# RWKV-7's triangular inverses: layouts turned on VectorE instead of through DRAM, with a new order and new engines around them

## The chip, the cores and the metric

One core of a Trainium2 chip runs the whole program. The metric is the device time of one execution in microseconds (us); a kernel's time is the median of its runs. The profile comes from one further execution, with its own time.

## What is computed

Two blocks of two layers each, in 32-bit floats: 512 tokens, 1024 features. The first layer, and only that one is touched here, joins a convolution branch `ya` and an RWKV-7 branch `yb`:

```python
z = h @ even_w_in
a_val, a_glu, a_gate, r, k, v, wd, ad, b_gate = split_cols(z, EVEN_SIZES)
ya = conformer_conv(a_val, a_glu, ...) * silu(a_gate)   # 31 taps, layer norm over 1024 features
yb = rwkv7_mix(r, k, v, wd, ad, ...) * silu(b_gate)     # 16 heads of 64
out = concatenate([ya, yb], axis=-1) @ even_w_out
x = x + gate[:, None, :] * out

def rwkv7_step(state, inp):                             # scanned over the 512 tokens
    r_t, w_t, k_t, v_t, kk_t, a_t = inp
    sa = einsum('bhvk,bhk->bhv', state, -kk_t)
    state = state * w_t + sa * (kk_t * a_t) + v_t * k_t
    y = einsum('bhvk,bhk->bhv', state, r_t)
```

After it come a sparse attention layer, an LRU layer and a forgetting attention layer, which stay as they are.

## The kernel before

**Projections.** Nearly all of TensorE's work is weight products. Each 128x128 weight tile times 128x512 activations is done as three matmuls, by a high and a low part of both factors (`mm3`, L168 to L170): `wh` times `h` (the activations' high part), `wh` times their low part, `wl` times `h`. The raw tile `wr` comes by an SP DMA (L133). ScalarE makes `wh` (L145) and minus `wr` (L146), and a DMA on POOL's queue adds `wr` in memory to give `wl` (L147). `wh` and `wl` have four buffers each. `K.fill` yields such products in steps of three matmuls, so that they can be laid between other work.

**The RWKV branch** is a scan over 8 chunks of 64 tokens, for 8 heads at a time: half 0 (H0), then half 1 (H1). Each half has four stages. `prep` makes decayed queries and keys `AR` and `BK`. `inverse` needs, for each of the 64 pairs of head and chunk, the inverse of a unit triangular 64x64 matrix. `merge` puts its blocks together. `chunk`, eight times, carries the state on; TensorE gets projections to do beside it.

**The inverse** (L656 on). TensorE makes the 64x64 products N (L669, four PSUM banks). VectorE multiplies each bank by the mask `gmask` (L671) and the result goes to DRAM. From there DMAs bring the two 32x32 diagonal blocks of each matrix back as `Nu`, with matrices along the partitions (L675), and the block off the diagonal as `No` (L677). VectorE then solves by forward substitution in 31 steps, each a product and a sum in two pieces (L688, L689): a chain in which each instruction needs the last. The solution `Yu` goes to DRAM. A copy of its first 64 partitions, blocks transposed (L691), goes there as well. From DRAM, `merge` loads `Yt` (L703) and `X11` (L705) in the layout that TensorE needs: rows of a block along the partitions. All these DMAs are on SP's queue. Then come, for 32 matrices at a time, 32x32 products (L714), a ScalarE copy (L717), further products (L719) and a copy into `Yt` (L720).

**Around it.** `ahead` prepares a chunk's matrices: masked products G (L729, L731), V transposed (L736, L739), and for all chunks but the last the keys scaled by the decay `PC`, one POOL product of 128x512 (L745), four TensorE transposes and a ScalarE copy (L748, L750). `conv_stats` (L880 on), laid beside H1's inverse, subtracts the mean from eight tiles (POOL, L888), squares them (ScalarE, L890), sums the squares (POOL, L894), and multiplies the sum by ones for the deviation (L898, L899; reciprocal L904). Beside it, the products of the finished `yb` with `even_w_out` run as a fill (evacuated at L964), for which `yb` is split into high and low parts (L971, and on POOL L972). The other half, the products with `ya`, needs H1's merge behind it in TensorE's order.

**What sets the order.** The program is written in one order, and a scheduler of the tile framework reorders it by a simulated timeline and by priorities (`K.later` lowers the priority of what stands in it, `issue_after` ties it behind an instruction). Tiles come from pools with a count of buffers per tag (`q4` has three here). Engines run their own instructions in the order that results, and wait on semaphores.

Of the kernel before, what the change touches and what calls it, by code (L numbers as in the profile page):

```python
# [10 lines left out]
F = mybir.dt.float32  # L11
# [4 lines left out]
OP = mybir.AluOpType  # L16
# [443 lines left out]
def even_layer(K, ada1):  # L460
# [12 lines left out]
    with K.layer("even", {"mm": (0, 1), "t": (2, 3, 4), "u": (5, 6), "ada": (7,), "py": (7,)}, s=6, k=4, v=4, q4=3, no=1, Yt=1, BKt=2, SAV=2, U=3, cu=2, fg=3, mean=2, awa=1, pa=1):  # L473
        xT, hT = [], []
        ss = SumSq(K, tags=("s", "cu"), eng=nc.vector)
        for i in range(ND):
# [89 lines left out]
        class Half:  # L566
# [91 lines left out]
            def inverse(self):  # L658


                AR, BK = self.AR, self.BK
                No, Nu = K.t("no", (P, 4 * NCH, 32)), K.t("q4", (P, 32, 32))
                n = K.name("sp")
                nd = K.dram.tile([P, 4 * NCH, C], F, name=n, tag=n)
                for j in range(4):
                    p = K.ps("t")
                    for c in range(NCH):
                        for b in range(2):
                            mm(p[hs(b), c * C:(c + 1) * C], lhsT=BK[hs(b), j, c, b], rhs=AR[hs(b), j, c, 0], start=True, stop=True)  # L669
                    n = K.t(shape=(P, NCH, C))  # L670
                    nc.vector.tensor_tensor(out=n, in0=v3(p), in1=gmask[:, None, 0:C].to_broadcast([P, NCH, C]), op=OP.mult)  # L671
                    nc.sync.dma_start(out=nd[:, NCH * j:NCH * j + NCH], in_=n)
                quarters = [(b, q, 64 * b + 32 * q, slice(64 * q + 32 * b, 64 * q + 32 * b + 32)) for b in range(2) for q in range(2)]
                for b, q, r, o in quarters:
                    nc.sync.dma_start(out=Nu[o], in_=nd[r:r + 32, :, 32 * q:32 * q + 32].rearrange("a u b -> u a b"))  # L675
                    if q == 0:
                        nc.sync.dma_start(out=No[r:r + 32], in_=nd[r:r + 32, :, 32:64])  # L677
                Yu, pr = K.t("q4", (P, 32, 32)), K.t("q4", (P, 32, 32))
                nc.gpsimd.memset(Yu, 0.0)
                nc.gpsimd.memset(Yu.rearrange("p a b -> p (a b)")[:, 0::33], 1.0)  # L680

                for b in range(31):
                    for eng, r0, r1 in ((nc.vector,0,8),(nc.vector,8,32)):
                        if b >= r0:
                            a = slice(r0, min(b + 1, r1))
                            sh = [P, a.stop - r0, 31 - b]
                            z = pr[:, a, b + 1:]
                            eng.tensor_tensor(out=z, in0=Yu[:, a, b:b + 1].to_broadcast(sh), in1=Nu[:, b:b + 1, b + 1:].to_broadcast(sh), op=OP.mult)  # L688
                            eng.tensor_tensor(out=Yu[:, a, b + 1:], in0=Yu[:, a, b + 1:], in1=z, op=OP.add)  # L689
                Yd = K.spill(Yu)  # L690
                self.last = nc.vector.tensor_copy(pr[0:64], Yu[0:64].rearrange("p a b -> p b a"))  # L691
                Xd = K.spill(pr[0:64])
                self.ahead(0, K.t("SAV", (P, 2, 4, C)))
                self.parts = No, Yd, Xd, quarters

            def merge(self, fill=()):

                No, Yd, Xd, quarters = self.parts
                Yt = self.Yt = K.t("Yt", (P, 4 * NCH, C))
                X11 = K.t("q4", (P, 4 * NCH, 32))  # L700
                for b, q, r, o in quarters:
                    f = lambda d, o: d[o].rearrange("u a b -> a u b")
                    nc.sync.dma_start(out=Yt[r:r + 32, :, 32 * q:32 * q + 32], in_=f(Yd, o))  # L703
                    if q == 0:
                        nc.sync.dma_start(out=X11[r:r + 32], in_=f(Xd, o))  # L705
                    else:
                        nc.gpsimd.memset(Yt[r:r + 32, :, 0:32], 0.0)
                for u in range(0, 4 * NCH, 16):
                    p, p2 = K.ps("t"), K.ps("t")
                    o1 = K.t(shape=(P, 16, 32))  # L710
                    for b in range(2):
                        r, r2 = slice(64 * b, 64 * b + 32), slice(64 * b + 32, 64 * b + 64)
                        for c in range(16):
                            i = mm(p[r2, 32 * c:32 * c + 32], lhsT=No[r, u + c], rhs=X11[r, u + c], start=True, stop=True)  # L714
                        if fill:
                            K.steps(fill, 2, i.ins)
                        nc.scalar.copy(o1[r2], p[r2].rearrange("p (c t) -> p c t", t=32))  # L717
                        for c in range(16):
                            mm(p2[r, 32 * c:32 * c + 32], lhsT=o1[r2, c], rhs=Yt[r2, u + c, 32:64], start=True, stop=True)  # L719
                        nc.scalar.copy(Yt[r, u:u + 16, 32:64], p2[r].rearrange("p (c t) -> p c t", t=32))  # L720

            def ahead(self, c, SAV):
# [18 lines left out]
                if c < NCH - 1:  # L741

                    bk = K.t(shape=(P, 4, P))
                    pcb = self.PC[:, :, c].unsqueeze(2).to_broadcast([P, 4, P])
                    nc.gpsimd.tensor_tensor(out=bk, in0=BK[:, :, c].rearrange("p j a t -> p j (a t)"), in1=pcb, op=OP.mult)  # L745
                    p = K.ps("t")
                    for j in range(4):
                        nc.tensor.transpose(p[:, j * P:(j + 1) * P], bk[:, j], K.ident)  # L748
                    BKt = K.t("BKt", (P, 8, C))
                    nc.scalar.copy(BKt, v3(p))  # L750
# [127 lines left out]
        def conv_stats():  # L878
# [77 lines left out]
        with K.later():  # L956
# [706 lines left out]
```

## Time and profile before

| | |
|---|---|
| Median of 3 runs | 1786.72 us (1777.45 to 1789.82) |
| The profiled execution's own time | 1791.05 us |
| its span, first to last instruction | 1789.3 us |
| TensorE busy | 1657.9 us (93%) |
| VectorE / ScalarE / POOL busy | 1142.2 / 1090.4 / 637.6 us |
| mean granted TensorE clock | 0.955 of full |

TensorE is busy for nearly all of the span, so what is not its own work is found as its gaps, and as the stretches in which it is granted a lower clock. All times inside the span count from its start. In a row of the timeline, the bracket at the end is the time that the engine sat idle before the instruction and what ended it. A row with xN stands for N instructions in sequence.

### The profile page before, as it was taken

To read this page: it belongs to the slowest core of one execution; us is meant where nothing else is said; L and a number is where in the kernel's file an instruction comes from. 1 tells how busy PE (TensorE), PEld (TensorE's weight loads), DVE (VectorE), ACT (ScalarE), POOL (GpSimd) and SP (SyncE) were. 2 spreads that over 40 slices of the span, in tenths; PEclk is the share of its full clock that TensorE was granted. 3 is DMA by queue.
4 is the path that set the end of the run, shared out by engine and by line. 5 is a ranking of instruction groups with operands and counts; after the bars stand their busy time and mean duration, and the time that the engine had idled before them with its cause. 6 is when DMAs were issued, how large, how long until landed. Compare 5 with 4: busy or idle time off the path is not lost.

```text
span 1789.3 us, 26544 instructions
## 1 busy us (share of the span) xinstructions
PE 1657.9 (93%) x9250; PEld 1310.1 (73%) x9250; DVE 1142.2 (64%) x2247; ACT 1090.4 (61%) x2106; POOL 637.6 (36%) x678
## 2 busy tenths in 40 slices
PE   5899999998995999888999899999999999999997
PEld 4676777776664777767887688888788777877775
DVE  6489776795948567456968878922688621454442
ACT  3574545445554435478565678765789755776775
POOL 1244423233566212133323445332333333333332
PEclk9899997898998989899999999999999999999999
DMA  9866894446678976476879741078777798865654
GB/s 284 211 147 163 184 215 110 107 95 174 153 179 193 273 219 151 119 170 142 179 168 229 197 89 35 18 166 193 165 177 167 150 190 190 199 143 138 154 109 116
DMA packets 164087, 289.19 MB, mean 162 GB/s; under 512 B 43985, under 2 KB 60753, under 8 KB 162929
## 3 DMA queue, kind: packets, MB, share of 16 engines
q0 software_dynamic: 60352, 107.24, 35.7%
q1 hardware_dynamic: 99568, 172.91, 30.9%
q10 hardware_dynamic: 4032, 7.34, 1.1%
q8 instruction: 73, 1.20, 0.3%
q14 instruction: 62, 0.50, 0.1%
HBM read 162.10 MB, written 18.12 MB: 101 GB/s over the span
## 4 chain that ended last, share of the span: by engine, by line
PE 59%; DVE 13%; DMA 12%; issue 8%; ACT 3%; POOL 3%; SPq 1%; POOLq 0%; DVEq 0%; ACTq 0%
PE ps L168 15%; PE ps L169 15%; PE ps L170 15%; DVE x L859 4%; DMA wl<-wr 3%; DMA wr<-in_even_w_in 2%; POOL wl L147 1%; DMA adm<-in_ada_w 1%; PE ps L1525 1%; PE ps L729 1%; DMA sp<-gt 1%; PE ps L1521 1%; PE ps L550 1%; PE ps L1261 1%; POOL mean L894 1%
## 5 line engine op out<-in xcount | busy, mean ns | idle before, releaser
L147 POOL DMA_DIRECT2D wl<-wr x416 | 364.7, 882 | 871.6 <-ACT wl L146 772.3
L170 PE MATMUL ps<-h,wl 128*128 128x512 f32 x1240 | 498.8, 406 | 29.4 <-DMA wl<-wr 29.0
L168 PE MATMUL ps<-h,wh 128*128 128x512 f32 x1240 | 508.5, 415 | 18.7 <-ACT h L332 6.8
L169 PE MATMUL ps<-h,wh 128*128 128x512 f32 x1240 | 500.0, 405 | 0.1
L145 ACT CAST wh<-wr 128x512 fp32r<-128x512 f32 (+1 forms) x416 | 251.9, 606 | 355.6 <-PE ps L169 253.8
L170 PEld LDWEIGHTS ps<-h,wl 128*128 128x128 f32 x1240 | 241.0, 195 | 91.0 <-DMA wl<-wr 37.5
L168 PEld LDWEIGHTS ps<-h,wh 128*128 128x128 f32 x1240 | 243.4, 197 | 83.3 <-ACT h L332 8.3
L169 PEld LDWEIGHTS ps<-h,wh 128*128 128x128 f32 x1240 | 242.0, 195 | 52.7 <-issue 2.7
L146 ACT ACTIVATE wl<-wr 128x512 fp32r<-128x512 f32 (+1 forms) x416 | 256.5, 617 | 28.0 <-PE ps L169 26.5
L859 DVE SCALAR_TENSOR_TENSOR x<-cu,vec,x 128x512 f32<-128x512 f32 x216 | 185.9, 862 | 4.9
L1258 POOL TENSOR_SCALAR pp<-pp,st 128x512 f32<-128x512 f32 x32 | 52.2, 1632 | 68.9 <-DVE st L1254 58.8
L1253 ACT ACTIVATE pp<-pp,st 128x512 f32<-128x512 f32 x64 | 46.2, 722 | 18.2 <-DVE st L1252 18.0
L1515 DVE CUSTOM_DVE_ANT_0 pp<-ps,nb 128x128 f32<-128x128 f32 (+3 forms) x64 | 30.6, 488 | 30.3 <-PE ps L1510 21.8
L169 PE MATMUL ps<-wl,h 128*128 128x512 f32 x120 | 47.6, 398 | 0.7 <-DMA wl<-wr 0.7
L1252 DVE CUSTOM_DVE_ANT_0 pp<-ps,bias 128x512 f32<-128x512 f32 x64 | 43.6, 681 | 6.4 <-PE ps L1261 6.0
L170 PE MATMUL ps<-wh,h 128*128 128x512 f32 x120 | 46.5, 393 | 0.0
L688 DVE TENSOR_TENSOR q<-q,q 128x112 f32<-128x112 f32 (+25 forms) x108 | 27.2, 288 | 29.2 <-DMA q<-sp 28.8
L168 PE MATMUL ps<-wh,h 128*128 128x512 f32 x120 | 45.4, 405 | 0.0
L288 ACT CAST pT<-ps 128x512 fp32r<-128x512 f32 x64 | 36.4, 577 | 14.1 <-PE ps L1261 13.6
L1518 POOL TENSOR_SCALAR pp<-pp,st 128x128 f32<-128x128 f32 (+1 forms) x32 | 32.0, 1032 | 36.5 <-DVE st L1517 36.4
L289 DVE TENSOR_TENSOR pT<-ps,pT 128x512 fp32r<-128x512 f32 x64 | 43.3, 680 | 0.8 <-ACT pT L288 0.7
L1188 DVE MATCH_REPLACE8 acc<-m,acc 128x512 f32<-128x512 f32 x64 | 42.8, 674 | 0.0
(522 smaller groups left out, 3332.1 us busy)
## 6 DMA issues: line engine op xcount, KB each, us to landing
wl<-wr POOLq DMA_DIRECT2D x376, 256.0 KB, 4.1
wr<-in_even_w_in SPq DMA_DIRECT2D x50, 512.0 KB, 4.1
wr<-in_odd_w_in SPq DMA_DIRECT2D x39, 512.0 KB, 4.2
wr<-in_lru_w_in SPq DMA_DIRECT2D x24, 512.0 KB, 3.8
wr<-in_fox_w_qkg SPq DMA_DIRECT2D x24, 512.0 KB, 4.4
k<-in_ada_w SPq DMA_DIRECT2D x32, 256.0 KB, 3.9
wr<-in_odd_w_out SPq DMA_DIRECT2D x16, 512.0 KB, 4.0
wl<-wr POOLq DMA_DIRECT2D x40, 192.0 KB, 4.1
```

The lines of the kernel that those rows point to most:

```text
L145: nc.scalar.copy(h, raw)
L146: nc.scalar.mul(l, raw, -1.0)
L147: nc.gpsimd.dma_start(out=l, in_=raw, accum_op=OP.add)
L168: mm(ps, lhsT=w[0], rhs=x[0], start=first, stop=False)
L169: mm(ps, lhsT=w[0], rhs=x[1], start=False, stop=False)
L170: self.last_mm = mm(ps, lhsT=w[1], rhs=x[0], start=False, stop=last).ins
L289: nc.vector.tensor_tensor(out=l, in0=src, in1=h.bitcast(F), op=OP.subtract)
L859: nc.vector.scalar_tensor_tensor(out=acc, in0=u[:, q:q + S], scalar=w[q], in1=acc, op0=OP.mult, op1=OP.add)
L1188: nc.vector.match_replace(out=acc, in_to_replace=m8, in_values=acc, imm_value=TAKEN)
L1252: nc.vector.tensor_tensor_reduce(out=pp, in0=lg, in1=bias[t], scale=1.0, scalar=3e38, op0=OP.add, op1=OP.min, accum_out=mx)
L1253: nc.scalar.activation(pp, pp, AF.Exp, scale=-1.0, bias=mx, accum_out=sm)
L1258: (nc.vector if t % 2 else nc.gpsimd).tensor_scalar(out=pp, in0=pp, scalar1=sm, scalar2=None, op0=OP.mult)
```

## The change

1. N no longer goes through DRAM. ScalarE copies each PSUM bank into `Yt` without the mask (the substitution reads only entries behind the diagonal). Three block transposes on VectorE (L676 of the kernel after; 32x32 blocks within 32 partitions) bring the diagonal blocks into `Nu`.
2. The solution comes back by a transpose into `X11` (L687) and three into `Yt` (L689), on VectorE. The spills, the loads and the copy L691 go. The block off the diagonal is read from `Yt` itself. POOL clears the lower left blocks when the merge begins.
3. The first chunk's `ahead` and, for H0, the projections of the fourth convolution tile (`conv_in(3)`) are written ahead of the merge's matmuls.
4. The keys' decay moves from one POOL product to four ScalarE products of 128x128 (L735).
5. `conv_stats` sums its squares on VectorE (L882) instead of POOL.
6. The low part of `yb` is made by ScalarE (times -1) and an adding DMA on POOL's queue (L961) instead of a POOL subtraction.

Lines of the kernel after are up to 12 lower than before from here on: the merge's products are L703 and L708, G's are L718 and L720, the first product of a chunk L758 (L770 before).

```diff
                 for j in range(4):
                     p = K.ps("t")
                     ...
-                    n = K.t(shape=(P, NCH, C))
-                    nc.vector.tensor_tensor(out=n, in0=v3(p), in1=gmask[:, None, 0:C].to_broadcast([P, NCH, C]), op=OP.mult)
-                    nc.sync.dma_start(out=nd[:, NCH * j:NCH * j + NCH], in_=n)
-                for b, q, r, o in quarters:
-                    nc.sync.dma_start(out=Nu[o], in_=nd[r:r + 32, :, 32 * q:32 * q + 32].rearrange("a u b -> u a b"))
-                    if q == 0:
-                        nc.sync.dma_start(out=No[r:r + 32], in_=nd[r:r + 32, :, 32:64])
+                    nc.scalar.copy(Yt[:, NCH * j:NCH * j + NCH], v3(p))
+                quarters = [(q, slice(64 * b + 32 * q, 64 * b + 32 * q + 32)) for q in range(2) for b in range(2)]
+                turn = nc.vector.transpose
+                for q, r in [(0, slice(0, P))] + quarters[2:]:
+                    turn(out=Nu[r].rearrange("u a b -> u b a"), in_=Yt[r, :, 32 * q:32 * q + 32].rearrange("a u b -> a b u"))
...
-                Yd = K.spill(Yu)
-                self.last = nc.vector.tensor_copy(pr[0:64], Yu[0:64].rearrange("p a b -> p b a"))
-                Xd = K.spill(pr[0:64])
+                X11 = self.X11 = K.t("q4", (P, 32, 32))
+                turn(out=X11.rearrange("p u a -> p a u"), in_=Yu)
+                for q, r in quarters[2:] + [(0, slice(0, P))]:
+                    self.last = turn(out=Yt[r, :, 32 * q:32 * q + 32].rearrange("p u b -> p b u"), in_=Yu[r].rearrange("u a b -> u b a"))
+            def merge(self, fill=()):
+                for b in range(2):
+                    nc.gpsimd.memset(Yt[64 * b + 32:64 * b + 64, :, 0:32], 0.0)
                 self.ahead(0, K.t("SAV", (P, 2, 4, C)))
...
-                            i = mm(p[r2, 32 * c:32 * c + 32], lhsT=No[r, u + c], rhs=X11[r, u + c], start=True, stop=True)
+                            i = mm(p[r2, 32 * c:32 * c + 32], lhsT=Yt[r, u + c, 32:64], rhs=X11[r, u + c], start=True, stop=True)
...
-                    nc.gpsimd.tensor_tensor(out=bk, in0=BK[:, :, c].rearrange("p j a t -> p j (a t)"), in1=pcb, op=OP.mult)
                     for j in range(4):
+                        nc.scalar.mul(bk[:, j], BK[:, j, c].rearrange("p a t -> p (a t)"), self.PC[:, j, c:c + 1])
                         nc.tensor.transpose(p[:, j * P:(j + 1) * P], bk[:, j], K.ident)
...
-                    nc.gpsimd.tensor_tensor(out=acc, in0=acc, in1=sq[:, :S], op=OP.add)
+                    nc.vector.tensor_tensor(out=acc, in0=acc, in1=sq[:, :S], op=OP.add)
...
+        conv_in(3)
         H0.merge()
-        conv_in(3)
...
-                nc.gpsimd.tensor_tensor(out=l, in0=y, in1=h.bitcast(F), op=OP.subtract)
+                nc.scalar.mul(l, y, -1.0)
+                nc.gpsimd.dma_start(out=l, in_=y, accum_op=OP.add)
```

The change moves instructions on three engines. First TensorE where H1's merge begins, before: the two products L714 behind the last of `yb`'s projections of their bank (`q` is X11, `no` the block off the diagonal).

```order
L168 MATMUL ps_4795<-h_4733,wh_4773 128x512
L169 MATMUL ps_4795<-h_4734,wh_4773 128x512
L170 MATMUL ps_4795<-h_4733,wl_4774 128x512
L714 MATMUL ps_4885<-q_4876,no_4149 32x32 x16
L714 MATMUL ps_4981<-q_4876,no_4149 32x32 x16
L168 MATMUL ps_4820<-h_4715,wh_4798 128x512
```

And the same place now (`q_4339` is X11, `q_4839` is G of the first chunk, `s_4861` the scaled keys).

```order
L169 MATMUL ps_4731<-h_4694,wh_4709 128x512
L170 MATMUL ps_4731<-h_4693,wl_4710 128x512
L736 MATMUL ps_4862<-ident,s_4861 128x128 x4
L758 MATMUL ps_5142<-SAV_4838,q_4839 64x64
L703 MATMUL ps_4873<-q_4339,Yt_4150 32x32 x16
L758 MATMUL ps_5142<-SAV_4838,q_4839 64x64 x7
L703 MATMUL ps_4969<-q_4339,Yt_4150 32x32 x16
```

From the last N product to the merge stood 164 projection matmuls, now 140; for H0 some 212, now 157. A matmul with G of the first chunk now stands ahead of the merge's.

Next POOL beside H1's substitution, before: sums of squares (L894) between the low parts of weights (L147), the scaled keys (L745) and the identity's clearing (L679).

```order
L888 TENSOR_TENSOR x_3875<-x_3875,mean_4430 128x512
L894 TENSOR_TENSOR mean_4433<-mean_4433,cu_4436 128x512
L147 DMA wl_4549<-wr_4546 128x512
L745 TENSOR_TENSOR s_4378<-BK_3569,PC_3570 128x512
L679 MEMSET q_4238 128x1024
L147 DMA wl_4554<-wr_4546 128x512
L894 TENSOR_TENSOR mean_4433<-mean_4433,cu_4440 128x512
```

And now, behind the same last subtraction (L876).

```order
L876 TENSOR_TENSOR x_3876<-x_3876,mean_4387 128x512
L147 DMA wl_4506<-wr_4503 128x512
...
L147 DMA wl_4702<-wr_4699 128x512
L147 DMA wl_4710<-wr_4707 128x512
L961 DMA h_4673<-k_4671 128x512
L961 DMA h_4680<-k_4678 128x512
```

Ten low parts of weights stand in a row, with no sum between them, and the four low parts of `yb` behind them as DMAs.

Last VectorE ahead of H1's substitution, now (before, the four L671 and then L688 stood there).

```order
L882 TENSOR_TENSOR mean_4390<-mean_4390,cu_4413 128x512
L676 STREAM_TRANSPOSE q_4223<-Yt_4150 128x32x32
L882 TENSOR_TENSOR mean_4390<-mean_4390,cu_4417 128x512
L676 STREAM_TRANSPOSE q_4223<-Yt_4150 32x32x32 x2
L684 TENSOR_TENSOR q_4225<-q_4224,q_4223 128x31
```

And at its end, now (before, two L731, then the copy L691 and the reciprocal L904).

```order
L685 TENSOR_TENSOR q_4224<-q_4224,q_4225 128x8
L687 STREAM_TRANSPOSE q_4339<-q_4224 128x32x32
L689 STREAM_TRANSPOSE Yt_4150<-q_4224 32x32x32 x2
L689 STREAM_TRANSPOSE Yt_4150<-q_4224 128x32x32
L720 TENSOR_TENSOR q_4839<-ps_4840,gmask_541 128x4x128
```

All seven sums of squares stand ahead of the substitution, the four turns back between it and the first chunk's G.

## Rows read from the trace of the kernel before

**Rows 1.** The profile's page: busy time by engine; the chain's shares; POOL's costliest line.

```profile
PE 1657.9 (93%) x9250; PEld 1310.1 (73%) x9250; DVE 1142.2 (64%) x2247; ACT 1090.4 (61%) x2106; POOL 637.6 (36%) x678
...
PE 59%; DVE 13%; DMA 12%; issue 8%; ACT 3%; POOL 3%; SPq 1%; POOLq 0%; DVEq 0%; ACTq 0%
...
L147 POOL DMA_DIRECT2D wl<-wr x416 | 364.7, 882 | 871.6 <-ACT wl L146 772.3
```

**Rows 2.** Timeline of TensorE, H1's inverse and merge (start, duration, ..., idle before).

```profile
514.69 2.08 PE L669 MATMUL ps<-AR,BK 64*64 64x64 f32 x62
...
554.89 0.79 PE L170 MATMUL ps<-h,wl 128*128 128x512 f32 x1 [10.93 <-DMA wl<-wr]
...
566.38 0.50 PE L168 MATMUL ps<-h,wh 128*128 128x512 f32 x1 [0.64 <-ACT mean L899]
...
572.54 0.50 PE L168 MATMUL ps<-h,wh 128*128 128x512 f32 x1 [0.74 <-DVE k L964]
...
581.38 3.59 PE L714 MATMUL ps<-q,no 32*32 32x32 f32 x64 [5.82 <-issue]
...
600.87 0.50 PE L168 MATMUL ps<-h,wh 128*128 128x512 f32 x1
```

**Rows 3.** Timeline of POOL beside H1's substitution.

```profile
511.16 9.99 POOL L888 TENSOR_TENSOR x<-x,mean 128x512 f32<-128x512 f32 x8
521.11 1.26 POOL L894 TENSOR_TENSOR mean<-mean,cu 128x512 f32<-128x512 f32 x1
...
536.64 0.86 POOL L147 DMA_DIRECT2D wl<-wr  x1 [2.86 <-ACT wl L146]
537.26 12.65 POOL L894 TENSOR_TENSOR mean<-mean,cu 128x512 f32<-128x512 f32 x1
549.86 0.86 POOL L147 DMA_DIRECT2D wl<-wr  x1
```

**Rows 4.** Timeline of TensorE, H0's inverse and merge.

```profile
208.68 1.15 PE L669 MATMUL ps<-AR,BK 64*64 64x64 f32 x32
...
238.93 0.50 PE L170 MATMUL ps<-h,wl 128*128 128x512 f32 x1 [2.63 <-DMA wl<-wr]
...
270.87 3.59 PE L714 MATMUL ps<-q,no 32*32 32x32 f32 x64 [3.15 <-issue]
```

**Rows 5.** Timeline of SP's DMA queue beside H0's inverse.

```profile
217.95 3.67 SPq L675 DMA_DIRECT2D q<-sp  x2
...
226.37 7.33 SPq L133 DMA_DIRECT2D wr<-in_even_w_in  x3
```

**Rows 6.** Windows: us, busy by engine (x instructions), TensorE's clock, DMA share, GB/s.

```profile
555.00:560.50 5.50, 5.50 (x13) 4.34 (x14) 5.16 (x14) 3.44 (x7) 3.19 (x3) 0.50 1.06 232
271.00:281.00 10.00, 9.87 (x83) 8.73 (x83) 7.00 (x11) 4.80 (x9) 1.82 (x2) 0.51 0.70 207
291.00:301.00 10.00, 10.00 (x74) 9.12 (x74) 4.87 (x9) 3.30 (x6) 2.48 (x3) 0.50 0.26 64
578.00:588.00 10.00, 6.62 (x71) 5.97 (x72) 6.28 (x8) 5.08 (x9) 1.96 (x2) 0.50 1.09 305
516.80:543.96 27.16, 27.16 (x126) 21.86 (x126) 14.29 (x56) 14.72 (x27) 24.30 (x19) 1.00 0.85 188
209.80:236.30 26.50, 26.25 (x120) 20.96 (x118) 10.54 (x40) 13.72 (x25) 9.86 (x13) 1.00 0.97 217
```

**Rows 7.** Timeline of VectorE: H0's substitution, first and last row; H1's first; the reciprocal.

```profile
230.29 0.28 DVE L688 TENSOR_TENSOR q<-q,q 128x31 f32<-128x31 f32 x2 [15.89 <-DMA q<-sp]
...
251.55 0.18 DVE L689 TENSOR_TENSOR q<-q,q 128x8 f32<-128x8 f32 x1
...
530.40 1.38 DVE L688 TENSOR_TENSOR q<-q,q 128x31 f32<-128x31 f32 x2 [12.87 <-DMA q<-sp]
...
566.36 3.35 DVE L904 RECIPROCAL mean<-mean 128x512 f32<-128x512 f32 x1 [4.64 <-ACT mean L899]
```

**Rows 8.** All instructions of two VectorE lines (ns: min/median/max, starts, forms).

```profile
L671 DVE TENSOR_TENSOR s<-ps,gmask x8: 680/684/692, 192.5 to 516.9; 128x512 f32<-128x512 f32 x8
L691 DVE COPY q<-q x2: 1114/2232/3350, 252.8 to 558.4; 64x1024 f32<-64x1024 f32 x2
```

**Rows 9.** Groups by line and form (busy us, mean ns | idle before).

```profile
L745 POOL TENSOR_TENSOR s<-BK,PC 128x512 f32<-128x512 f32 x14 | 15.8, 1233 | 5.6 <-PE ps L719 5.4
L739 ACT COPY SAV<-ps 64x256 f32<-64x256 f32 x32 | 11.7, 365 | 6.6 <-PE ps L736 6.1
L750 ACT COPY BKt<-ps 128x512 f32<-128x512 f32 x14 | 8.1, 580 | 4.6 <-PE ps L748 3.1 <-PE ps L790 1.3
```

More of the change, by code (lines that the diff above doesn't have):

```diff
@@ L472, in even_layer @@
     A = Ada(K, 0)
-    with K.layer("even", {"mm": (0, 1), "t": (2, 3, 4), "u": (5, 6), "ada": (7,), "py": (7,)}, s=6, k=4, v=4, q4=3, no=1, Yt=1, BKt=2, SAV=2, U=3, cu=2, fg=3, mean=2, awa=1, pa=1):
+    with K.layer("even", {"mm": (0, 1), "t": (2, 3, 4), "u": (5, 6), "ada": (7,), "py": (7,)}, s=6, k=4, v=4, q4=3, Yt=1, BKt=2, SAV=2, U=3, cu=2, fg=3, mean=2, awa=1, pa=1):
         xT, hT = [], []
@@ L661, in inverse @@
                 AR, BK = self.AR, self.BK
-                No, Nu = K.t("no", (P, 4 * NCH, 32)), K.t("q4", (P, 32, 32))
-                n = K.name("sp")
-                nd = K.dram.tile([P, 4 * NCH, C], F, name=n, tag=n)
+                Yt = self.Yt = K.t("Yt", (P, 4 * NCH, C))
                 for j in range(4):
@@ L669, in inverse @@
                             mm(p[hs(b), c * C:(c + 1) * C], lhsT=BK[hs(b), j, c, b], rhs=AR[hs(b), j, c, 0], start=True, stop=True)
-                    n = K.t(shape=(P, NCH, C))
-                    nc.vector.tensor_tensor(out=n, in0=v3(p), in1=gmask[:, None, 0:C].to_broadcast([P, NCH, C]), op=OP.mult)
-                    nc.sync.dma_start(out=nd[:, NCH * j:NCH * j + NCH], in_=n)
-                quarters = [(b, q, 64 * b + 32 * q, slice(64 * q + 32 * b, 64 * q + 32 * b + 32)) for b in range(2) for q in range(2)]
-                for b, q, r, o in quarters:
-                    nc.sync.dma_start(out=Nu[o], in_=nd[r:r + 32, :, 32 * q:32 * q + 32].rearrange("a u b -> u a b"))
-                    if q == 0:
-                        nc.sync.dma_start(out=No[r:r + 32], in_=nd[r:r + 32, :, 32:64])
-                Yu, pr = K.t("q4", (P, 32, 32)), K.t("q4", (P, 32, 32))
+                    nc.scalar.copy(Yt[:, NCH * j:NCH * j + NCH], v3(p))
+                quarters = [(q, slice(64 * b + 32 * q, 64 * b + 32 * q + 32)) for q in range(2) for b in range(2)]
+                turn = nc.vector.transpose
+                Nu, Yu, pr = (K.t("q4", (P, 32, 32)) for _ in range(3))
                 nc.gpsimd.memset(Yu, 0.0)
                 nc.gpsimd.memset(Yu.rearrange("p a b -> p (a b)")[:, 0::33], 1.0)
+                for q, r in [(0, slice(0, P))] + quarters[2:]:
+                    turn(out=Nu[r].rearrange("u a b -> u b a"), in_=Yt[r, :, 32 * q:32 * q + 32].rearrange("a u b -> a b u"))
                 for b in range(31):
@@ L689, in inverse @@
                             eng.tensor_tensor(out=Yu[:, a, b + 1:], in0=Yu[:, a, b + 1:], in1=z, op=OP.add)
-                Yd = K.spill(Yu)
-                self.last = nc.vector.tensor_copy(pr[0:64], Yu[0:64].rearrange("p a b -> p b a"))
-                Xd = K.spill(pr[0:64])
-                self.ahead(0, K.t("SAV", (P, 2, 4, C)))
[L694 to L707, printed above, removed]
+                X11 = self.X11 = K.t("q4", (P, 32, 32))
[3 more added lines that the diff above has]
+            def merge(self, fill=()):
+                Yt, X11 = self.Yt, self.X11
+                for b in range(2):
+                    nc.gpsimd.memset(Yt[64 * b + 32:64 * b + 64, :, 0:32], 0.0)
+                self.ahead(0, K.t("SAV", (P, 2, 4, C)))
                 for u in range(0, 4 * NCH, 16):
@@ L743, in ahead @@
                     bk = K.t(shape=(P, 4, P))
-                    pcb = self.PC[:, :, c].unsqueeze(2).to_broadcast([P, 4, P])
-                    nc.gpsimd.tensor_tensor(out=bk, in0=BK[:, :, c].rearrange("p j a t -> p j (a t)"), in1=pcb, op=OP.mult)
                     p = K.ps("t")
                     for j in range(4):
+                        nc.scalar.mul(bk[:, j], BK[:, j, c].rearrange("p a t -> p (a t)"), self.PC[:, j, c:c + 1])
                         nc.tensor.transpose(p[:, j * P:(j + 1) * P], bk[:, j], K.ident)
```

## The prediction

> **What bounds the kernel now.** I read the page first: TensorE is busy for 93% of the span and has 59% of the chain that ended last; no other engine passes 64% [rows 1]. The change removes no work of TensorE worth naming, so a gain must come from its gaps, or from the clock. I therefore went through TensorE's timeline from the last N product of each half to the end of its merge, and then through the timelines of whatever released the gaps there.
>
> In H1 four gaps stand between the N products and the first product with `ya`: 10.93, 0.64, 0.74 and 5.82 us, 18.1 together [rows 2]. The long one is put down to a DMA, the low part of a weight. Its cause lies further back, on POOL: that DMA was to be issued at about 537, but the sum L894 ahead of it took 12.65 us where an earlier one took 1.26, so the trigger came at 549.86 [rows 3]. L894 sat beside VectorE's substitution all that time. The wait of 5.82 "issue" stands at the merge's first product, which needs what SP's queue loads last. H0 has two gaps, 2.63 and 3.15 us [rows 4]. There SP was busy with the layout loads (3.67 us for two of them), and three weight loads queued behind them took 7.33 to issue [rows 5].
>
> Behind these gaps the clock stood at the lower of its two levels (1.2 of 2.4 GHz): 0.50 at 555 to 560.5, 0.51 at 271 to 281, 0.50 at 578 to 588. It also stood there from 291 to 301, where TensorE had been running small matmuls with no such gap in front [rows 6].
>
> **The change part by part.** *The way through DRAM.* Before, VectorE stood idle for 15.89 us (H0) and 12.87 us (H1) until `Nu` was loaded [rows 7]. Now a ScalarE copy of each bank (0.58 for 128x512 out of PSUM [rows 9]) and three block transposes replace that. The trace has no block transpose. The nearest row by size and pattern is the copy L691, 1024 elements per partition with transposed blocks: 1.11 us in H0, 3.35 in H1 beside POOL's subtractions [rows 8]. That first figure is the lower end too: no row of this size is quicker, and a quicker turn would only add to the cover worked out below. From above, the dearest VectorE row per column is the reciprocal, 3.35 for 512 [rows 7], which is 6.7 for 1024. I take 1.11, since nothing but DMA triggers stands on POOL then, and keep 6.7 as the other end.
>
> *Does the substitution end before TensorE arrives?* For H0: the last N product ends at 209.8 [rows 4]; a copy of 0.6 and three turns make 213.7; the substitution itself took 251.7 - 230.3 = 21.4 [rows 7], so 235.1; then four turns and one masked product (0.68, as L671 [rows 8]) stand ahead of what TensorE needs: 240.2. TensorE has 169 matmuls to do up to there, of which 157 are projections. At 26.5/120 = 0.221 each [rows 6] they last 37.3 us, so it arrives at 247.1, 6.9 us later. For H1: the last N product stands 12 projections later, 516.8 + 2.6 = 519.4, and the 152 matmuls behind it, at 27.16/126 = 0.216 [rows 6], last 32.8: arrival at 552.2. VectorE starts when the last sum is there: POOL's subtractions end at 521.1 [rows 3], plus a square of about 0.6 and a sum of 0.68, plus the last two turns, 2.2: 524.6. Plus 21.4 makes 546.0, and 5.1 as above, 551.1. That leaves 1.1 us, little cover: with the 6.9 of H0, all fourteen turns may together cost 8 us more before TensorE waits longer by the whole of it. I expect the waits at both merges (5.82 and 3.15) to go.
>
> *POOL's sums to VectorE.* Seven sums at 0.68 are 4.8 us for VectorE, which also loses eight L671 of 0.68 (5.4): nothing in sum. With no sum on POOL, nothing can hold a trigger for 12 us, and the 10.93 goes. The two small gaps (0.64, 0.74) hang on the deviation and on the evacuation behind the same block, and go with it. H0's 2.63 goes if the weight loads no longer queue behind layout loads; that is the least sure of the six.
>
> *Clock.* Half of each lower stretch that follows a removed gap could come back: 2.75 of 5.5, 4.9 of 9.87, 3.3 of 6.62 busy [rows 6], 11 in all. The first merge still holds small matmuls, and 291 to 301 shows them at the low level with no gap in front. So I count 6.
>
> *Keys by ScalarE.* 14 POOL products of 1.23 [rows 9] become 56 ScalarE products of 128 columns. ScalarE took 0.58 for 512 columns and 0.365 for 256 [rows 9], a line that gives 0.26 for 128: 14.6 us, bounded by a quarter of 0.58 and by 0.365 at 8.1 and 20.4. In a step the four in sequence take 1.03, less than the 1.23 that the transposes waited for before. With eight copies of 0.58 ScalarE gains 19 us in work, part of it ahead of the casts of weights that TensorE needs next. I charge a fifth, 4 us; the ends are 0 (ScalarE has 39% idle) and 19.
>
> *Low part of `yb`.* The DMA (L961) stands on POOL behind ten weight triggers; each of the four costs a trigger of 0.88 [rows 1] and its landing instead of a subtraction. TensorE needs the last just ahead of the merge. I take it as hidden by the projections between, at most 3 us if it isn't.
>
> The Trainium skill (SBUF, State Buffer, section "Who interferes with whom") says that a VectorE instruction with two SBUF inputs contends with a GpSimd (POOL) instruction that reads SBUF, and that whichever issues second is blocked until the first ends. By that rule L894's 12.65 beside the substitution is explained, and the trace agrees (12.65 against 1.26 [rows 3]). It also speaks against the change: the sums now on VectorE have two SBUF inputs and run beside POOL's eight subtractions, on which H1's substitution now waits. Seven times 0.68 of blocking would be up to 4.8 us, of which 1.1 is covered, so the sum would end some 3 to 4 us later, near 1765 (an estimate from that rule).
>
> *The sum*, against the profiled execution: 1791.05 - 18.1 - 5.8 - 6 + 4 = 1765.1. The median of the runs stands 4.3 below that execution, so 1760.8: **1761 us**.
>
> **Rivals.** *Half of it.* The long gap goes, and H0's, but the cover at H1's merge isn't there (a substitution slowed as H1's was before, when its first two products alone took 1.38 instead of 0.28 [rows 7]) and L961 comes late: 3 us each. The clock then stays down. 1791.05 - 10.9 - 5.8 + 6 - 4.3 = 1776. For it speaks the cover of 1.1 us; against it, that POOL's reads, which stretched that row, are gone.
>
> *More.* All 11 of the clock's stretches come back, 5 more of those 10 us from 291 to 301, and ScalarE's new work is hidden: 1791.05 - 18.1 - 5.8 - 11 - 5 - 4.3 = 1747. For it: ScalarE has idle time; against it: the small matmuls stay, and with them what stood in front of the low clock there.
>
> *Nothing.* The gaps come back in other places, behind a weight that is late in any case (ScalarE's casts sit idle for what TensorE frees): about 1785.
>
> *Slower: dear transposes.* VectorE's turns are the mechanism, the place is the head of both merges. Each half has seven in sequence, three ahead of the substitution and four behind it, all ahead of TensorE's first matmul with G. At a price of p each, the waits are 14 (p - 1.11) - 8. At 3.5 us each that eats the 26 us of forecast gain; at 4.8 the kernel is slower by over 1%; at 6.7, the reciprocal's rate, it waits 70 us more, 1831. For it: no row shows one. Against it: the copy with the same pattern at 1.11, and only its worst instance at 3.35, near the point of no gain.
>
> **How the numbers follow.** About 1% (17.9 us) is what a measurement of this kernel can tell from no change. Forecast (gain of 18 to 34) 0.50; more, 0.17; half, 0.23; nothing, 0.05; dear transposes, 0.05, all of it slower. Faster by over 1% is the first two, 0.67; within 1% the half and nothing, 0.28; slower 0.05. The range runs from 1738, 9 below the case of more, which is as much as its two least sure terms (5 of the clock, 4 of ScalarE) could miss again, to 1782, which holds the half and leaves out the dear transposes and most of nothing.
>
> **What would show it.** Right: no L894-like row on POOL beside the substitution and no gap above 3 us at a product with `wl` between H1's N products and its merge; TensorE's first merge product without a wait, near 247 and, less what H0 gained, 552; the first product with `ya` some 24 us earlier than 600.87 [rows 2]; transposes near 1.1 us. Wrong: STREAM_TRANSPOSE rows above 2 us, with a gap at L758 released by G's mask L720; subtractions L876 stretched beside the sums; a gap at the last products of `yb` released by L961; ScalarE's casts late behind the products L735 in the chunk steps.

## The result, and the profile after

The kernel after took 1758.94 us (median of four runs, 1754.94 to 1762.15), where the kernel before took 1786.72. The ratio is 0.985, with a 95% interval of 0.982 to 0.988: faster by 27.8 us by the medians (ratios here and below are of means, so they need not be the quotients of medians). The forecast was 1761, with a range of 1738 to 1782. The profiled executions lie 34 us apart (1791.05 and 1757.27), since the one of before lies above its three runs and the one of after in the lower half of its own.

First the page of after, the lines that answer to [rows 1].

```profile
span 1755.1 us, 26518 instructions
...
PE 1646.0 (94%) x9250; PEld 1299.9 (74%) x9250; DVE 1158.7 (66%) x2258; ACT 1114.1 (63%) x2174; POOL 606.3 (35%) x657
```

TensorE does the same 9250 matmuls. Most of the gain is in one place: the last matmul of L550, behind the first layer, starts at 734.3 before and at 701.0 after, 33.3 us earlier, and the ends lie 34.2 apart. (In a second profile of the kernel after it starts at 706.7, 27.6 earlier, and the ends lie 33.7 apart.) So nearly everything, or at least four fifths, was won in the first layer, whose scan fills the time from 190 to 640. The next rows are windows over that stretch, first of before, then of after, then of that second profile of the kernel after (columns as in [rows 6]).

```profile
190.00:640.00 450.00, 401.68 (x2947) 310.36 (x2945) 328.23 (x594) 215.99 (x400) 181.89 (x181) 0.89 0.70 172
```
```profile
190.00:640.00 450.00, 422.67 (x3210) 327.07 (x3209) 370.00 (x653) 249.72 (x492) 155.77 (x168) 0.94 0.69 173
```
```profile
190.00:640.00 450.00, 424.81 (x3147) 328.69 (x3146) 363.08 (x642) 243.97 (x481) 153.07 (x165) 0.91 0.67 169
```

Two things are to be read here. TensorE's idle time fell from 450 - 401.7 = 48.3 us to 27.3 and 25.2, by 21 to 23. And the granted clock rose from 0.89 to 0.94, but in the second execution of the same program only to 0.91. Summed over windows of 5 us of the same view, TensorE was busy at the lower of its two levels for 78 us before, for 51 and 70 after. Half of the difference is time won: 14 us in the one execution and 4 in the other.

These windows end at the same time, not at the same work. The next ones end with the last matmul of L550, behind the same 4376 matmuls:

```profile
0.00:734.50 734.50, 647.22 (x4376) 498.31 (x4376) 521.04 (x911) 356.14 (x664) 268.08 (x284) 0.91 0.71 176
```
```profile
0.00:701.20 701.20, 635.12 (x4376) 487.59 (x4376) 538.09 (x922) 378.76 (x732) 235.90 (x263) 0.95 0.70 177
```
```profile
0.00:706.90 706.90, 643.31 (x4376) 494.43 (x4376) 537.77 (x922) 379.03 (x732) 233.90 (x263) 0.93 0.69 175
```

Here idle time fell from 87.3 us to 66.1 and 63.6, by 21 and 24, and the same matmuls were busy for 12 and 4 us less. So the idle time explains most of the gain and repeats. The clock's part differs between executions, and with one profile of before it can't be told how much of it belongs to the change. The two executions of the kernel after took the same time in all (1757.27 and 1757.71): what the second was late with in the first layer it made up behind it.

TensorE's timeline of after, at the places of [rows 2] and [rows 4]:

```profile
249.82 0.73 PE L736 MATMUL ps<-ident,s 128*128 128x128 f32 x4 [2.02 <-DVE q L720]
...
492.60 0.79 PE L168 MATMUL ps<-h,wh 128*128 128x512 f32 x1 [4.66 <-ACT fg L863]
...
538.08 0.50 PE L168 MATMUL ps<-h,wh 128*128 128x512 f32 x1 [3.05 <-ACT fg L863]
...
540.03 0.50 PE L169 MATMUL ps<-h,wh 128*128 128x512 f32 x1 [0.76 <-DMA h<-k]
541.77 0.79 PE L169 MATMUL ps<-h,wh 128*128 128x512 f32 x1 [0.40 <-DMA h<-k]
...
546.73 0.60 PE L736 MATMUL ps<-ident,s 128*128 128x128 f32 x4
...
552.21 1.75 PE L708 MATMUL ps<-Yt,s 32*32 32x32 f32 x29 [1.77 <-ACT s L706]
...
574.42 0.50 PE L168 MATMUL ps<-h,wh 128*128 128x512 f32 x1
```

All six gaps of before are gone. New ones stand at H0's merge (2.02, behind the mask product L720, which follows the turns), behind ScalarE (4.66 and 3.05), behind the adding DMAs (0.76 and 0.40) and inside H1's merge (1.77), 12.7 us together. H1's merge begins without a wait. The last row is the first product with `ya`: 26.5 us earlier than its 600.87 in [rows 2].

VectorE's transposes, all instructions by line:

```profile
L676 DVE STREAM_TRANSPOSE q<-Yt x6: 2158/2242/2271, 212.4 to 512.8; 32x1024 f32<-32x1024 f32 x4, 128x1024 f32<-128x1024 f32 x2
```
```profile
L687 DVE STREAM_TRANSPOSE q<-q x2: 1956/2030/2103, 240.2 to 536.1; 128x1024 f32<-128x1024 f32 x2
```
```profile
L689 DVE STREAM_TRANSPOSE Yt<-q x6: 2220/2261/2329, 242.3 to 542.6; 32x1024 f32<-32x1024 f32 x4, 128x1024 f32<-128x1024 f32 x2
```

A turn takes 2.0 to 2.3 us, twice the 1.11 that I took, and as long on 32 partitions as on 128.

VectorE's first and last row of H1's substitution, which took 535.91 + 0.17 - 515.11 = 20.97 us (H0's 20.98):

```profile
515.11 0.29 DVE L684 TENSOR_TENSOR q<-q,q 128x31 f32<-128x31 f32 x2
...
535.91 0.17 DVE L685 TENSOR_TENSOR q<-q,q 128x8 f32<-128x8 f32 x1
```

### The profile page after: what moved, and what is told of

The parts are those of the page before. It is cut to its first block, busy times and chain, and to the rows that moved or that the text cites. A ratio compares the mean times of both kernels' runs of the same rounds, so it can differ in the third digit from the quotient of the medians.

```text
span 1755.1 us, 26518 instructions
## 1 busy us (share of the span) xinstructions
PE 1646.0 (94%) x9250; PEld 1299.9 (74%) x9250; DVE 1158.7 (66%) x2258; ACT 1114.1 (63%) x2174; POOL 606.3 (35%) x657
## 4 chain that ended last, share of the span: by engine, by line
PE 58%; DVE 15%; DMA 12%; issue 8%; ACT 4%; POOL 2%; SPq 0%; POOLq 0%; ACTq 0%; DVEq 0%
PE ps L168 15%; PE ps L169 15%; PE ps L170 15%; DVE x L847 4%; DMA wl<-wr 3%; DMA wr<-in_even_w_in 2%; DMA k<-in_ada_w 1%; PE ps L718 1%; PE ps L1514 1%; POOL wl L147 1%; DMA adm<-in_ada_w 1%; DMA sp<-gt 1%; PE ps L1510 1%; ACT wh L145 1%; PE ps L1250 1%
## 5 line engine op out<-in xcount | busy, mean ns | idle before, releaser
L147 POOL DMA_DIRECT2D wl<-wr x416 | 363.7, 879 | 877.1 <-ACT wl L146 801.1
L146 ACT ACTIVATE wl<-wr 128x512 fp32r<-128x512 f32 (+1 forms) x416 | 257.0, 618 | 29.5 <-PE ps L169 27.8
L847 DVE SCALAR_TENSOR_TENSOR x<-cu,vec,x 128x512 f32<-128x512 f32 x216 | 180.1, 836 | 4.8
L169 PE MATMUL ps<-wl,h 128*128 128x512 f32 x120 | 48.3, 403 | 2.4 <-DMA wl<-wr 2.4
L1511 ACT COPY pT<-ps 128x128 f32<-128x128 f32 (+3 forms) x64 | 25.9, 419 | 27.6 <-PE ps L1510 27.4
```

The costliest lines, as they stand in the source:

```text
L146: nc.scalar.mul(l, raw, -1.0)
L147: nc.gpsimd.dma_start(out=l, in_=raw, accum_op=OP.add)
L169: mm(ps, lhsT=w[0], rhs=x[1], start=False, stop=False)
L847: nc.vector.scalar_tensor_tensor(out=acc, in0=u[:, q:q + S], scalar=w[q], in1=acc, op0=OP.mult, op1=OP.add)
```

## The experiments

Theory A was that of the prediction: POOL's sums, held up beside the substitution, hold weight triggers and so TensorE, and the way through DRAM costs the waits at the merges. Theory B said that the way through DRAM is the whole of it. Beside them stood the questions whether ScalarE's new work costs time, and what the turns cost. One half of part 3, the first chunk's `ahead` written ahead of the merge, was never undone by itself. Medians below are set beside the kernel before of the same rounds (1785 to 1787).

**1. The sums alone moved, in the kernel before.**

```diff
-                    nc.gpsimd.tensor_tensor(out=acc, in0=acc, in1=sq[:, :S], op=OP.add)
+                    nc.vector.tensor_tensor(out=acc, in0=acc, in1=sq[:, :S], op=OP.add)
```

> The kernel before with only the sums of squares moved from POOL to VectorE; the layout still goes through DRAM. Theory A (the long gap is POOL's sum held up beside VectorE's substitution, with weight triggers queued behind it): the gap of 10.93 us at a product with wl goes, the merge's 5.82 stays or grows, since TensorE reaches the merge earlier while the DRAM loads don't come earlier; 4 to 12 us faster than before, 1775 to 1783. Theory B (the gain is the way through DRAM alone): no change, 1785 to 1789.

It took 1780.04 against 1785.11 (ratio 0.998, interval 0.996 to 1.001). The difference can't be told from none, though the median lies where A put it. TensorE's timeline says why:

```profile
552.77 0.50 PE L168 MATMUL ps<-h,wh 128*128 128x512 f32 x1 [3.80 <-ACT fg L875]
...
565.33 0.79 PE L168 MATMUL ps<-h,wh 128*128 128x512 f32 x1 [3.86 <-DVE k L964]
...
574.31 1.17 PE L714 MATMUL ps<-q,no 32*32 32x32 f32 x32 [2.24 <-issue]
```

The gap of 10.93 is gone, as A had it (1.33 and 0.92 are left at products with `wl`). But the substitution still starts late, at 532.4, behind the loads, and ends at 558.4. TensorE, no longer held by the weights, runs into evacuations that ScalarE (L875) and VectorE (L964) make late, and then into the merge: 12.2 us in these five gaps, where 18.1 stood in four. What one wait gave up, others took. In H0, too, whose layout still came through DRAM, gaps of 2.14 and 2.13 us stayed where 2.63 and 3.15 had stood; the kernel after has one of 2.02 in their place.

**2. The layout and the order alone: keys, sums and low parts of `yb` back on POOL.**

```diff
-                        nc.scalar.mul(bk[:, j], BK[:, j, c]..., self.PC[:, j, c:c + 1])
+                    nc.gpsimd.tensor_tensor(out=bk, in0=BK[:, :, c]..., in1=pcb, op=OP.mult)
...
-                    nc.vector.tensor_tensor(out=acc, in0=acc, in1=sq[:, :S], op=OP.add)
+                    nc.gpsimd.tensor_tensor(out=acc, in0=acc, in1=sq[:, :S], op=OP.add)
...
-                nc.scalar.mul(l, y, -1.0)
-                nc.gpsimd.dma_start(out=l, in_=y, accum_op=OP.add)
+                nc.gpsimd.tensor_tensor(out=l, in0=y, in1=h.bitcast(F), op=OP.subtract)
```

> The kernel after with keys, sums and low parts of yb back on POOL (parts 4, 5 and 6 undone), so the layout by transposes and the order alone. Theory A: the sums are again held beside the substitution and hold weight triggers, a gap of 5 to 11 us returns ahead of H1's merge: 1766 to 1772. Theory B: 1757 to 1762, as the kernel after.

1766.19 (0.990; 0.987 to 0.993), at the lower end of A's range; the interval, some 1761 to 1773, touches B's, so the trace has to decide. In it the gap is back: 10.21 us at a product with `wl`, released by that weight's DMA, with one of POOL's sums at 11.67 us ahead of the trigger. POOL's row, and TensorE's:

```profile
527.73 11.67 POOL L883 TENSOR_TENSOR mean<-mean,cu 128x512 f32<-128x512 f32 x1
```
```profile
544.49 0.79 PE L170 MATMUL ps<-h,wl 128*128 128x512 f32 x1 [10.21 <-DMA wl<-wr]
```

**3. The kernel after with only the sums back on POOL.**

> The kernel after with only the sums of squares back on POOL. Theory A: POOL's sums last 2 us or more each beside the substitution, one of them many times that, and a gap at a product with wl returns: 1764 to 1771. Theory B: within 3 us of the kernel after (1756 to 1762), even a little quicker, since the sums no longer stand ahead of the substitution on VectorE (7 x 1.17 us there).

1772.23 (0.994; 0.992 to 0.996), a little above A's range, and 13 us above the kernel after; B, which had no loss, falls. POOL's timeline, and then TensorE's:

```profile
519.64 1.59 POOL L882 TENSOR_TENSOR mean<-mean,cu 128x512 f32<-128x512 f32 x1
...
528.37 12.15 POOL L882 TENSOR_TENSOR mean<-mean,cu 128x512 f32<-128x512 f32 x1
540.47 2.64 POOL L147 DMA_DIRECT2D wl<-wr  x3
```
```profile
545.37 0.79 PE L170 MATMUL ps<-h,wl 128*128 128x512 f32 x1 [9.98 <-DMA wl<-wr]
```

This is [rows 3] once more, without the way through DRAM: three triggers are issued as soon as the held sum ends, and TensorE starts when the first has landed. The substitution itself took 26.4 us here, 21.0 in the kernel after. The sums that weren't held took 1.5 to 1.9 us, less than the 2 that A expected.

**4. The kernel after with the keys back on POOL.** (The first edit of experiment 2.)

> The kernel after with only the scaling of the keys back on POOL (14 products of 1.23 us instead of 56 of ScalarE). Theory A, which charged ScalarE's added work: 2 to 5 us faster than the kernel after, 1754 to 1757. Rival C (the keys' products on POOL stand among the weight triggers and delay them, and in a chunk step the four small products let the transposes start sooner): 2 to 6 us slower than the kernel after, 1761 to 1765.

1763.94, with runs from 1752.6 to 1767.9 (0.989; 0.984 to 0.993): too wide to tell it from the kernel after, though the median lies in C's range. Experiment 10 asks again.

**5. The kernel after with the low parts of `yb` back on POOL.** (The last edit of experiment 2.)

> The kernel after with only the low parts of yb back as POOL subtractions. Kernel after shows two gaps of 0.76 and 0.40 us released by the adding DMA and a gap of 3.05 us behind ScalarE, which does the four products of 0.63 us in that place. Theory A (that place is paced by ScalarE): the gaps of 3.05, 0.76 and 0.40 shrink to 1 or 2 us in all; 2 to 4 us faster than the kernel after, 1755 to 1757. Rival D (POOL's subtractions, which read SBUF, are held up beside the substitution and hold the weight triggers behind them): a gap of 5 us or more comes back, 1762 to 1768.

1767.78 (0.988; 0.983 to 0.994). The median lies in rival D's range, but the interval reaches into the kernel after's. No weight trigger was held. TensorE waited elsewhere:

```profile
557.57 1.12 PE L736 MATMUL ps<-ident,s 128*128 128x128 f32 x4 [6.66 <-DVE q L720]
```
```profile
537.44 2.86 POOL L960 TENSOR_TENSOR h<-k,h 128x512 fp32r<-128x512 f32 x2
541.62 2.79 POOL L960 TENSOR_TENSOR h<-k,h 128x512 fp32r<-128x512 f32 x2
```

The substitution took 26.74 us instead of 20.97, 5.77 longer, and POOL's four subtractions, which ran beside it, took 2.86 + 2.79 = 5.65. That is what the adding DMAs of part 6 avoid, at the price of two gaps of 0.76 and 0.40. These two were gone here, and the 3.05 behind ScalarE was 2.08, just above the 1 to 2 that A expected; the 6.66 at the merge, which neither theory had, outweighs them.

**6. The kernel after with `conv_in(3)` written behind H0's merge.**

```diff
-        conv_in(3)
         H0.merge()
+        conv_in(3)
```

> The kernel after with conv_in(3) written behind H0's merge again. Theory A (projections ahead of the merge cover H0's substitution and turns): TensorE reaches H0's merge earlier than VectorE's turns end, the gap of 2.02 us there grows by up to what the moved projections take (48 matmuls at 0.22 = 10.6 us), and the half-speed stretch behind it with it: 3 to 12 us slower than the kernel after. Rival (the scheduler places the projections by its own timeline, whatever the order written): within 2 us of the kernel after.

1756.72 (0.981; 0.977 to 0.986): not slower, so A's expectation falls. The scheduler lays 154 projection matmuls between the last N product and H0's merge, where it lays 157 with the order of after, and the gap at the merge was 0.96. The written order of this call does nothing here that can be measured.

**7. One turn back instead of three.**

```diff
-                for q, r in quarters[2:] + [(0, slice(0, P))]:
-                    self.last = turn(out=Yt[r, :, 32 * q:32 * q + 32].rearrange("p u b -> p b u"), in_=Yu[r].rearrange("u a b -> u b a"))
+                self.last = turn(out=Yt[:, :, 0:32].rearrange("p u b -> p b u"), in_=Yu.rearrange("u a b -> u b a"))
+                for q, r in quarters[2:]:
+                    nc.scalar.copy(Yt[r, :, 32:64], Yt[r, :, 0:32])
```

> The kernel after with one transpose of all 128 partitions instead of three behind the substitution; ScalarE copies the lower right blocks to their place (two copies of 32x1024). VectorE's path from the substitution to the first chunk's G gets 2 x 2.26 = 4.5 us shorter in each half. If the turns are on TensorE's path in H0 (its gap of 2.02 us) and hidden in H1 (no gap at the merge): the gap of 2.02 goes, 1 to 3 us faster than the kernel after. If TensorE waits for something else there: no change, or 1 to 2 us slower for the copies.

1753.30 (0.981; 0.978 to 0.984). H0's gap at the merge is gone. The median lies 5.6 below the kernel after's 1758.94, more than the 1 to 3 expected, but the intervals overlap; experiment 9 compares a like version in the same rounds.

**8. One turn on either side.** Beside the edit of 7:

```diff
                     nc.scalar.copy(Yt[:, NCH * j:NCH * j + NCH], v3(p))
+                    for r in (slice(32, 64), slice(96, 128)):
+                        nc.scalar.copy(Yt[r, NCH * j:NCH * j + NCH, 0:32], v3(p)[r, :, 32:64])
...
-                for q, r in [(0, slice(0, P))] + quarters[2:]:
-                    turn(out=Nu[r].rearrange("u a b -> u b a"), in_=Yt[r, :, 32 * q:32 * q + 32].rearrange("a u b -> a b u"))
+                turn(out=Nu.rearrange("u a b -> u b a"), in_=Yt[:, :, 0:32].rearrange("a u b -> a b u"))
```

> As the one before, and also one transpose of all 128 partitions instead of three ahead of the substitution: ScalarE writes the lower right blocks of N a second time where that transpose finds them (eight copies of 32x256 in each half). Another 4.4 us off VectorE's path in each half, 5.9 us of ScalarE's time more. If the turns bound the halves: 1 to 3 us faster than with the turns back alone. If ScalarE does by now (the kernel after's gaps of 4.66 and 3.05 us are released by it): 0 to 3 us slower than that.

1752.37 (0.981; 0.979 to 0.983): as 7.

**9. The kernel after and version 8 in the same rounds.**

> The kernel after, unchanged, on the same chip and in the same rounds as the three that follow, so that they can be compared with it and not only with the kernel before. Expected: 1755 to 1763.

> The version with one transpose of all 128 partitions on either side of the substitution, again, beside the kernel after. If the 9 us that it takes off VectorE's path in each half are what H0's gap of 2.02 us and the low clock behind it came from: 3 to 8 us faster than the kernel after in these rounds. If the two earlier results differed by chance: within 2 us of it.

1761.36 and 1753.88, against 1787.06 for the kernel before (ratios 0.986 and 0.982). The means of six runs each are 1760.5 and 1753.8; from their scatter (3.7 and 4.6 us) the difference is 6.7 us, give or take 5.4. So the version with one turn on either side beats both kernels, and four turns fewer in a half are worth 1 to 12 us. Where they are won isn't shown beyond H0's gap of 2.02, which is gone: up to the last matmul of L550, two profiles of version 8 (experiments 8 and 9) have TensorE idle for 62.2 and 68.3 us, and two of the kernel after for 66.1 and 63.6.

**10. Version 8 with the keys on POOL.** (The first edit of experiment 2.)

> The version with one transpose on either side, and the keys' scaling back on POOL (14 products of 1.23 us). If ScalarE's 56 products of 0.3 to 0.4 us cost TensorE time, as the prediction charged (4 us): 2 to 5 us faster than the version with ScalarE's keys. If they are hidden by ScalarE's idle time, or POOL's products among the weight triggers cost as much: within 2 us of it, or slower.

1756.72 (0.984; 0.981 to 0.987), beside 1753.88 with ScalarE's keys. ScalarE's products cost nothing that shows in the time, and there is no sign of a gain in moving them back.

**11. Work on POOL that nothing needs, beside the substitution.** After step 10 of the substitution, four sums in H0, eight clearings in H1:

```diff
+                    if b == 10:
+                        f = x[:, 256:257]
+                        nc.vector.tensor_copy(f, Yu[:, 0, b:b + 1])
+                        nc.gpsimd.tensor_copy(x[:, 0:1], f)
+                        ...
+                            if self.hf == 0:
+                                nc.gpsimd.tensor_tensor(out=x[:, 0:256], in0=self.AR[:, 0, 0:2]..., in1=self.BK[:, 0, 0:2]..., op=OP.add)
+                            else:
+                                nc.gpsimd.memset(x[:, 0:256], 0.0)
```

> The kernel after with work on POOL that nothing needs, started by a copy of one column after step 10 of the substitution: in H0 four sums of 128x256 that read two tiles in SBUF, in H1 eight clearings of 128x256 that only write. Undisturbed, both substitutions take 20.97 us. If reading SBUF is what holds VectorE and POOL up against each other: H0's substitution takes about 2.5 to 4 us longer (four times a sum's 0.65 to 0.9), H1's at most 0.3 us (the copy and one read of one column). If any POOL work beside it does: both grow alike, H1's by 2 us or more. If neither grows, what stretched the substitutions with sums beside them was something else.

VectorE's timeline gives the substitutions' first and last instructions, H0's and then H1's:

```profile
217.77 0.28 DVE L684 TENSOR_TENSOR q<-q,q 128x31 f32<-128x31 f32 x2
...
241.52 0.18 DVE L685 TENSOR_TENSOR q<-q,q 128x8 f32<-128x8 f32 x1
...
512.21 0.28 DVE L684 TENSOR_TENSOR q<-q,q 128x31 f32<-128x31 f32 x2
...
533.04 0.18 DVE L685 TENSOR_TENSOR q<-q,q 128x8 f32<-128x8 f32 x1
```

H0's took 23.93 us, 2.96 more than the 20.97 it takes undisturbed; the four sums lasted 3.50 (2.48 and 1.02). H1's took 21.01, beside eight clearings. POOL's timeline shows the other side:

```profile
225.74 7.18 POOL L690 COPY probe<-probe 128x1 f32<-128x1 f32 x1 [0.24 <-DVE probe L689]
233.01 2.48 POOL L693 TENSOR_TENSOR probe<-AR,BK 128x256 f32<-128x256 f32 x3
235.43 0.88 POOL L147 DMA_DIRECT2D wl<-wr  x1
```
```profile
520.19 7.50 POOL L690 COPY probe<-probe 128x1 f32<-128x1 f32 x1 [1.39 <-DVE probe L689]
527.74 1.05 POOL L695 MEMSET probe<- 128x256 f32 x3
```

A copy of one column, which reads SBUF, was held for more than 7 us in either half. Behind it, sums slow the substitution by nearly what they last, and clearings leave it as it was. A trigger between the sums took 0.88, as long as elsewhere (0.86).

TensorE's timeline has a gap in both halves, at products whose weights' triggers stood behind this work:

```profile
238.78 0.79 PE L170 MATMUL ps<-h,wl 128*128 128x512 f32 x1 [4.06 <-DMA wl<-wr]
...
532.34 0.80 PE L170 MATMUL ps<-h,wl 128*128 128x512 f32 x1 [6.77 <-DMA wl<-wr]
```

In H1 nothing but the held copy and clearings stood ahead of the trigger (529.01), and the kernel after has no gap at a product with `wl` there. This version ran once (1760.46 us, with no forecast of the time).

## Why the prediction was right, point by point

**The long gap and its cause: right, but not worth its length by itself.** The step that put 10.93 us to POOL's held sum is shown by experiments 2 and 3, where the gap returns at 10.21 and 9.98 behind a sum of 11.67 and 12.15, and by experiment 11, where a copy of one column does for the sum. What the prediction missed is that this gap and the late substitution stand one behind the other. The sums moved alone win 5 us that can't be told from none, the layout with POOL's work left as it was 19, both with the rest 28. Gaps on one chain may be added only if all their causes go at once, as they did here.

**The waits at the merges: right in total, in part by luck.** The sum took off 23.9 us of gaps and put back 4 for new ones, -19.9. Idle time between 190 and 640 fell by 21.0 in the profiled execution, 23.1 in the second. All six gaps went, but 12.7 us of new ones came, which leaves 11.2. The other 10 came from gaps that the prediction didn't count, such as these two in the chunk steps of before; why they went wasn't tried.

```profile
320.65 0.63 PE L748 MATMUL ps<-ident,s 128*128 128x128 f32 x4 [2.91 <-DVE q L731]
...
382.10 0.33 PE L770 MATMUL ps<-SAV,q 128*64 128x64 f32 x2 [1.90 <-DVE SAV L796]
```

**The 4 us charged to ScalarE: too small, and for another reason.** The keys' products were to cost it. They took more of ScalarE than estimated, 18.0 us in all where 14.6 were taken, within the bounds of 8.1 and 20.4:

```profile
L735 ACT ACTIVATE s<-BK,PC 128x128 f32<-128x128 f32 x56 | 18.0, 396 | 4.9 <-POOL BK L642 2.9 <-DMA sp<-s 1.7 <-DVE BK L641 0.2
```

Yet experiment 10 shows no cost of theirs in the time. The new waits behind ScalarE are 4.66 and 3.05, at evacuations that it makes late. Ahead of the first it had itself waited 3.96 us for a DMA, and then did three of the keys' products (0.97) and a copy of N (0.56) among other work; in experiment 6, with the same work there but a wait of only 0.29, the gap was 0.45. Ahead of the second, ScalarE's timeline has the casts and negations of `yb`, part 6; without the negations 2.08 of it stayed (experiment 5).

**The turns: the step that was mis-sized.** I took 1.11 us from a copy; they take 2.2. By the prediction's own formula 14 x (2.2 - 1.11) - 8 = 7 us of waits follow. What showed at the merges was 2.02, in H0 alone. In H1 TensorE itself came later, held by 3.05, 0.76 and 0.40 behind the last N product, and reached the merge at 546.73, when G's mask product had just ended (544.75 + 1.24 = 545.99). That H1 shows no wait is luck: other waits took its place. Experiment 9 puts the price of eight turns at 6.7 us, give or take 5.4. The rival of dear transposes had the mechanism right, and the price was below its point of no gain (3.5 us).

**The clock: a term that no single profile can check.** 6 us were counted. Over the same work, one execution gave 12 and another of the same kernel 4. The forecast lies between them.

**The sums beside POOL's subtractions.** The rule of the Trainium skill that was weighed (SBUF, State Buffer, "Who interferes with whom") is borne out in kind: the seven sums on VectorE took 1.17 us in the mean, and 0.70 once POOL's subtractions were done; those took 12.3 us instead of 9.99 [rows 3]. That a POOL instruction that only writes doesn't contend is shown by experiment 11. The loss of 3 to 4 us by that rule can't be told apart in the total. But the rule doesn't explain the 12.65 us of L894, as the prediction had it: blocked until the other's instruction ends would be some 0.3 us here (the longest rows of the chain take 0.55 for two), and the copy of experiment 11 was held over more than thirty of VectorE's instructions.

**Order.** That `conv_in(3)` stands ahead of the merge was read from the order of both kernels, and the count of 157 was right. It isn't the edit's doing, as experiment 6 shows: the scheduler arrives at nearly that without it.

**The signs.** Of the signs of being right, the held sum and the gap at `wl` went, and the first product with `ya` came 26.5 us earlier (24 forecast); the merge began without a wait in H1 alone. Of the four signs of being wrong, three showed: turns above 2 us with a gap released by L720, subtractions stretched beside the sums, and gaps released by L961. Together they were too small to take the time out of the range.

So the total was right within about 2 us. The main mechanism is shown. The errors of the other terms partly cancel: new gaps three times what was charged, about as much saved at places that weren't counted, turns twice as dear, the clock uncertain. What stays open is how much of the clock's part belongs to the change, and why the uncounted gaps shrank.

## What to carry to other kernels

When an instruction lasts ten times as long as its like, look at what ran beside it before looking at itself, and follow what is queued behind it on its engine. Here a sum on POOL beside a dense chain on VectorE held the triggers of weights' low parts, and by them TensorE. Remove the causes of gaps that follow one another together, or the next one takes over what the first gave up; and price an operation that the trace doesn't show by its worst neighbour as well as by its nearest.

## What was new of the hardware

- A POOL instruction that reads SBUF was held beside VectorE's chain of two-input products and sums not for one of VectorE's instructions but for many: a one-column copy for 7.18 and 7.50 us, sums for 11.7 to 12.7. Sums issued in the first 4 us of the chain got through in 1.5 to 2.1 us; the held ones were issued 6.9 to 9.2 us into it. All five (before, experiments 2 and 3, both halves of experiment 11) got through at the same step of the chain, the one with 96 columns, though that step came 15 to 20 us after the start. VectorE's rows at that place, of before, of experiment 3 and of H0 in experiment 11, are longer than the 0.43 that this row takes in the kernel after:

```profile
548.69 1.48 DVE L689 TENSOR_TENSOR q<-q,q 128x96 f32<-128x96 f32 x2
```
```profile
539.33 1.46 DVE L685 TENSOR_TENSOR q<-q,q 128x96 f32<-128x96 f32 x2
```
```profile
233.11 0.94 DVE L685 TENSOR_TENSOR q<-q,q 128x96 f32<-128x96 f32 x2
```

So what opens the way goes with the step and not with the time since the start. What it is in that step wasn't tried.
- A block transpose on VectorE of 1024 32-bit elements per partition, in these patterns, took 2.0 to 2.3 us, as long for 32 partitions as for 128.
